# Up-projection of an FFN with seven block products for eight, on one core of a Trainium2 chip

## The chip, the cores and the metric

The program runs on 1 core of one Trainium2 chip. The metric is the device time of one execution in microseconds. Five engines work side by side: TensorE (PE in the profile, its weight loads PEld), VectorE (DVE), ScalarE (ACT), GpSimd (POOL) and SyncE (SP, which here issues loads). Each carries out its own instructions in order; semaphores hold one back until another's result is there.

## The reference

One step of a trunk of two layers over 640 tokens, 512 latent ones and 128 of context. Each layer has a mixer (attention, mLSTM and spatial gating) and an FFN. The change is in the FFN, and in where the modulation vectors (shift, scale, gate) are computed:

```python
D_MODEL = 1024; D_FF = 2816
def dwconv3(x, w, b):
    T = x.shape[1]
    xp = jnp.pad(x, ((0, 0), (1, 1), (0, 0)))
    return xp[:, :T] * w[0] + xp[:, 1:T + 1] * w[1] + xp[:, 2:] * w[2] + b

def trunk_layer(x, cond, l, P, rope, ctx):
    mod = (jax.nn.silu(cond) @ P['w_mod'][l] + P['b_mod'][l])[:, None, :]
    sh1, sc1, g1, sh2, sc2, g2 = jnp.split(mod, 6, axis=-1)
    h = rmsnorm(x) * (1.0 + sc1) + sh1
    mix, ctx_out = token_mixer(h, l, P, rope, ctx)
    x = x + g1 * mix
    h = rmsnorm(x) * (1.0 + sc2) + sh2
    u = dwconv3(h @ P['w_up'][l], P['ffn_conv_w'][l], P['ffn_conv_b'][l])
    x = x + g2 * ((jax.nn.silu(u[..., :D_FF]) * u[..., D_FF:]) @ P['w_down'][l])
    return x, ctx_out
```

## The kernel before

Activations lie feature by token: 128 features on the partitions, 640 tokens along the free axis, eight such tiles for the 1024 features. Each float32 operand of a large product is split into a high part (rounded to the matmul's float32 form) and a low part (the rest), and a product is three matmuls: high by high, high by low, low by high. `mm` runs over the feature tiles, these three terms and two halves of 320 tokens, so an output tile of 128 rows takes 8 x 3 x 2 = 48 matmuls of 320 columns. `weights` loads a tile's weights (tag `raw`), lets ScalarE round them to `whi` (line 104), and GpSimd and VectorE in turn subtract to get `wlo` (line 105); there are three `raw` buffers and four each of `whi` and `wlo`.

The FFN's up-projection has 44 output tiles, two to each of 22 pairs `f` (one under SiLU, one that multiplies it). `up` makes a pair: 96 matmuls into two accumulators in PSUM, each read by `conv` (ScalarE's pass at line 181, and four `scalar_tensor_tensor` of VectorE at lines 183 and 185, for 511 and 127 columns, which read the accumulator `acc` and add into the SBUF tile `cw`). `glu` then applies SiLU (line 964), multiplies on GpSimd (line 965) and splits the product into `act` tiles (lines 114 and 115). After each of three groups of pairs (`FFN_PARTS`) the down-projection adds that group's share to the residual `x`.

A modulation part is 512 columns of `w_mod` times the two condition vectors: eight loads issued by ScalarE, 16 narrow matmuls (line 290), four transposes (line 310). `mod_turn` places a part between bulk matmuls. Before, six parts run in the first layer's mixer and fourteen in its FFN, which include those of the second layer.

The order of the instructions on each engine is set when the program is built, by a scheduler that goes by its own estimate of time; calls marked `pin` keep the order in which the code is written.

## Time and profile before

| | |
|---|---|
| median of 3 runs | 2408.47 us (2407.22 to 2408.69) |
| the profiled execution | 2406.03 us, its span 2404.2 us |
| TensorE busy | 2369.4 us (99%) |
| VectorE busy | 1129.8 us (47%) |
| ScalarE busy | 950.2 us (40%) |
| GpSimd busy | 670.4 us (28%) |

The span runs from the first instruction to the last. A busy time is the time in which the engine had at least one instruction running; matmuls overlap in its pipeline, so their mean duration (310 ns) is longer than the distance between two. An instruction that waits for a port of the memory counts as busy.

### The profile page before, as it was taken

What the parts mean: (1) busy time and instruction counts of PE and PEld (TensorE: products, weight loads), DVE (VectorE), ACT (ScalarE), POOL (GpSimd) and SP (SyncE); (2) the same over time, 40 slices, a digit from 0 to 9 for tenths busy, and PEclk for the clock granted to TensorE, in tenths of its full rate; (3) what the DMA queues carried; (4) which work ended last, traced back from release to release, by engine and by line L of the source; (5) the groups of instructions that cost most, each with busy time, mean ns of one, the idle gap of its engine ahead of it and who ended that gap; (6) DMA issues with size and microseconds to landing.
All of it is one profiled execution on the core that took longest, in us unless ns stands there. A gap on an engine that the chain in (4) does not pass through costs nothing.

```text
span 2404.2 us, 40627 instructions
## 1 busy us (share of the span) xinstructions
PE 2369.4 (99%) x16708; PEld 2314.0 (96%) x16708; DVE 1129.8 (47%) x2102; ACT 950.2 (40%) x1737; POOL 670.4 (28%) x486
## 2 busy tenths in 40 slices
PE   8999999999999999999999999999999999999998
PEld 7999999999998999989999999999999999999998
DVE  5455535555246423424453555365544454243444
ACT  4432325455345323323354323254553543232334
POOL 2312222333322322313313222323324133232231
PEclk9999999999999999999999999999999999999999
DMA  9331251112241455452232222211112322222222
GB/s 317 106 106 58 72 165 66 64 63 67 74 150 62 138 171 174 136 171 77 84 103 72 72 66 67 69 56 63 63 53 72 117 67 74 76 78 72 80 71 70
DMA packets 88761, 227.39 MB, mean 95 GB/s; under 512 B 9472, under 2 KB 23936, under 8 KB 88576
## 3 DMA queue, kind: packets, MB, share of 16 engines
q1 hardware_dynamic: 68992, 189.14, 24.0%
q10 hardware_dynamic: 19584, 35.66, 4.3%
q8 instruction: 131, 2.15, 0.4%
q14 instruction: 54, 0.44, 0.1%
HBM read 217.41 MB, written 7.35 MB: 93 GB/s over the span
## 4 chain that ended last, share of the span: by engine, by line
PE 95%; DVE 3%; ACT 1%; issue 0%; DMA 0%; SPq 0%; DVEq 0%; ACTq 0%; POOL 0%; POOLq 0%
PE acc L133 78%; PE acc L174 6%; PE ms L290 2%; PE ms L920 2%; PE ms L891 2%; PE ms L174 1%; PE ms L913 1%; PE ms L765 1%; PE ms L754 1%; PE ms L767 1%; DVE x L488 0%; PE ms L719 0%; PE ms L585 0%; PE ms L310 0%; DVE h L405 0%
## 5 line engine op out<-in xcount | busy, mean ns | idle before, releaser
L133 PE MATMUL acc<-h,whi 128*128 128x320 f32 x6464 | 1247.1, 311 | 8.9 <-DVE h L405 5.1
L133 PEld LDWEIGHTS acc<-h,whi 128*128 128x128 f32 x6464 | 1021.0, 188 | 26.4 <-DVE h L405 9.1
L105 POOL TENSOR_TENSOR wlo<-raw,whi 128x512 fp32r<-128x512 f32 (+1 forms) x298 | 390.3, 1310 | 1323.4 <-ACT whi L104 1308.6
L133 PE MATMUL acc<-h,wlo 128*128 128x320 f32 x3232 | 757.8, 310 | 0.0
L104 ACT CAST whi<-raw 128x512 fp32r<-128x512 f32 x596 | 365.1, 614 | 993.4 <-PE acc L133 724.5
L133 PEld LDWEIGHTS acc<-h,wlo 128*128 128x128 f32 x3232 | 545.6, 188 | 0.1
L105 DVE TENSOR_TENSOR wlo<-raw,whi 128x512 fp32r<-128x512 f32 (+1 forms) x298 | 241.3, 810 | 469.2 <-ACT whi L104 430.2
L133 PE MATMUL acc<-act,whi 128*128 128x320 f32 x1408 | 269.3, 310 | 0.0
L133 PEld LDWEIGHTS acc<-act,whi 128*128 128x128 f32 x1408 | 221.9, 188 | 5.9 <-issue 5.9
L133 PE MATMUL acc<-act,wlo 128*128 128x320 f32 x704 | 165.8, 310 | 0.0
L548 DVE SCALAR_TENSOR_TENSOR x<-acc,mod,x 128x128 f32<-128x128 f32 (+3 forms) x136 | 66.3, 526 | 190.8 <-PE acc L133 190.8
L133 PE MATMUL acc<-y,whi 128*128 128x320 f32 x768 | 150.7, 312 | 1.4 <-DVE y L118 1.4
L174 PE MATMUL acc<-whi,h 128*128 128x256 f32 x768 | 145.7, 284 | 0.0
L183 DVE SCALAR_TENSOR_TENSOR cw<-acc,vec,cw 128x511 f32<-128x511 f32 (+1 forms) x176 | 95.7, 544 | 98.4 <-ACT cw L181 97.1
L174 PEld LDWEIGHTS acc<-whi,h 128*128 128x128 f32 x768 | 123.1, 192 | 0.8 <-ACT v L817 0.8
L133 PEld LDWEIGHTS acc<-y,whi 128*128 128x128 f32 x768 | 121.4, 188 | 2.0 <-DVE y L118 1.9
L133 PEld LDWEIGHTS acc<-act,wlo 128*128 128x128 f32 x704 | 119.0, 188 | 0.0
L965 POOL TENSOR_TENSOR cw<-cw,cw 128x640 f32<-128x640 f32 x44 | 69.4, 1578 | 155.9 <-DVE cw L185 155.9
L174 PE MATMUL acc<-wlo,h 128*128 128x256 f32 x384 | 108.9, 284 | 0.0
L185 DVE SCALAR_TENSOR_TENSOR cw<-acc,vec,cw 128x511 f32<-128x511 f32 (+1 forms) x176 | 96.7, 550 | 6.1
L133 PE MATMUL acc<-y,wlo 128*128 128x320 f32 x384 | 90.2, 313 | 0.0
L899 ACT ACTIVATE wk<-ms,mx 128x640 f32<-128x640 f32 (+1 forms) x80 | 56.7, 709 | 75.0 <-DVE mx L897 73.1
(256 smaller groups left out, 2385.8 us busy)
## 6 DMA issues: line engine op xcount, KB each, us to landing
raw<-w_in_f SPq DMA_DIRECT2D x98, 512.0 KB, 3.3
raw<-w_up SPq DMA_DIRECT2D x88, 512.0 KB, 3.3
mw<-w_mod ACTq DMA_DIRECT2D x104, 256.0 KB, 5.6
raw<-w_down SPq DMA_DIRECT2D x32, 448.0 KB, 3.4
raw<-w_in_v SPq DMA_DIRECT2D x24, 512.0 KB, 3.7
raw<-w_branch SPq DMA_DIRECT2D x24, 512.0 KB, 3.3
mw<-w_mod SPq DMA_DIRECT2D x16, 512.0 KB, 8.8
raw<-w_out SPq DMA_DIRECT2D x16, 512.0 KB, 3.2
```

Source lines behind the costliest of these rows:

```text
L104: nc.scalar.copy(hi, raw[:, a:b])
L105: self.alt().tensor_sub(lo, raw[:, a:b], hi.bitcast(F32))
L133: ins = nc.tensor.matmul(acc[:, s], a[:, sl], b[:, s], start=k == 0 and i == 0, stop=k == last and i == 2)
L174: self.queue(nc.tensor.matmul(accs[b], a[:, bs], w[:, sl], start=first and b % 2 == 0, stop=last and (b % 2 == 1 or b == NB - 1)))
L183: nc.vector.scalar_tensor_tensor(dst[:, a + 1 : b], acc[:, a : b - 1], w0, dst[:, a + 1 : b], ALU.mult, ALU.add)
L185: nc.vector.scalar_tensor_tensor(dst[:, a : b - 1], acc[:, a + 1 : b], w2, dst[:, a : b - 1], ALU.mult, ALU.add)
L290: ins = nc.tensor.matmul(ps[j : j + 32, 0:width], self.cs[:, k, :], raws[k], start=k < 4, stop=k >= 4, tile_position=(0, j))
L548: self.nc.vector.scalar_tensor_tensor(x[:, a:b], acc[:, a:b], g[:, k, i : i + 1], x[:, a:b], ALU.mult, ALU.add)
L891: nc.tensor.matmul(ps[:, s : s + 320], st[:, qs], kk[:, s : s + 320], start=i == 0, stop=i == 1)
L899: nc.scalar.activation(e[:, 0:nk], ps[:, 0:nk], AF.Exp, bias=mx, scale=scale, accum_out=sm[:, j : j + 1])
L920: nc.tensor.matmul(po, at[:, c * P : (c + 1) * P], vv, start=c == 0, stop=c == n - 1)
L965: nc.gpsimd.tensor_mul(cs[0], cs[0], cs[1])
```

## The change

The pairs 3 to 21 of each layer (38 in all) are computed by Strassen's algorithm: the two output tiles, the two halves of the 1024 features and the two halves of the tokens make blocks of two by two, and seven block products of 4 x 3 = 12 matmuls of 320 columns (`quarter`) take the place of eight. The seven weight blocks are the tiles' quarters or sums of them (`ws`, made by VectorE and GpSimd), each split by `halves`; the token factors (`tx`) are made once in a layer by `token_factors`, from the normalized activations, while the pairs 1 and 2 are computed as before. The products are collected from PSUM into two SBUF tiles `cw`, and `conv` now reads these instead of the accumulators. The down-projections come after four groups of pairs instead of three, their first two tiles interleaved. No modulation part runs in an FFN any more: all stand in the mixers and the output projections. The layer's constants move to the mixer's memory pool.

```diff
-FFN_PARTS = ((0, 7), (7, 14), (14, 22))
+FFN_PARTS = ((0, 5), (5, 11), (11, 16), (16, 22))
...
+    def quarter(self, acc, w, xs, first, last):
+        nc = self.nc
+        hi, lo = w
+        for k, (xh, xl) in enumerate(xs):
+            sl = slice(k * P, (k + 1) * P)
+            for i, (a, b) in enumerate(((hi, xh), (hi, xl), (lo, xh))):
+                ins = nc.tensor.matmul(acc, a[:, sl], b, start=first and k == 0 and i == 0, stop=k == 3 and i == 2,
+                                       skip_group_check=not first)
+                self.queue(ins, True)
+
+    def halves(self, src, eng=None):
...
+        if eng is None:
+            nc.scalar.activation(hi, src, AF.Identity, scale=-1.0)
+            nc.vector.scalar_tensor_tensor(lo, src, -1.0, hi.bitcast(F32), ALU.mult, ALU.subtract)
+        else:
+            nc.scalar.copy(hi, src)
+            eng.tensor_sub(lo, src, hi.bitcast(F32))
+        return hi, lo
+
+    def seven_front(self, st, b):
+        nc, p = self.nc, st["p"]
+        (a11, a12), (a21, a22) = st["r"]
+        w1 = self.halves(a11, nc.vector)
+        w2 = self.halves(a12, nc.gpsimd)
+        s1, s2, s3 = (self.t(p, [P, 512], F32, "ws") for _ in range(3))
+        nc.vector.tensor_add(s1, a21, a22)
+        nc.gpsimd.tensor_add(s2, s1, a11)
+        nc.vector.tensor_add(s3, a11, a21)
+        st["s"] = s1, s2, s3
+        self.quarter(st["x"], w1, b["11"], True, False)
+        nc.scalar.copy(st["c"][0][:, 0:NHALF], st["x"])
+        self.quarter(st["y"], w2, b["21"], True, True)
+        nc.vector.tensor_add(st["c"][0][:, 0:NHALF], st["y"], st["c"][0][:, 0:NHALF])
+
+    def seven_mid(self, st, b):
...
+        w6 = self.halves(s2, nc.gpsimd)
+        w5 = self.halves(s1, nc.vector)
+        w7 = self.halves(s3, nc.gpsimd)
+        nc.gpsimd.tensor_add(s2, s2, a12)
+        self.quarter(x, w6, b["t2"], False, False)
+        nc.scalar.copy(c0[:, NHALF:NT], x)
+        self.quarter(z, w5, b["t1"], True, False)
+        self.quarter(x, w7, b["t3"], False, False)
+        nc.scalar.copy(c1[:, NHALF:NT], x)
+        nc.vector.scalar_tensor_tensor(c1[:, NHALF:NT], z, -1.0, c1[:, NHALF:NT], ALU.mult, ALU.subtract)
+
+    def seven_back(self, st, b):
...
+        w4 = self.halves(st["r"][1][1])
+        w3 = self.halves(st["s"][1], nc.gpsimd)
+        self.quarter(st["x"], w4, b["t4"], False, True)
+        nc.scalar.mul(c1[:, 0:NHALF], st["x"], -1.0)
+        self.quarter(st["z"], w3, b["22"], False, True)
+        nc.vector.tensor_add(c0[:, NHALF:NT], st["z"], c0[:, NHALF:NT])
+        return c0, c1
...
+        def make(k):
+            u0, u1 = u[k], u[k + 4]
+            f0, f1 = (self.t(p, [P, NHALF], F32, "ws") for _ in range(2))
+            (a0, a1, _), (p0, p1, _) = cols
+            self.tc.keep_in_program_order(nc.vector.tensor_sub(f0[:, a0], u0[:, a0], u0[:, a1]))
+            nc.vector.scalar_tensor_tensor(f0[:, p0], u0[:, p0], d0[:, k : k + 1], u0[:, p1], ALU.add, ALU.subtract)
+            for c0, c1, g in cols:
+                nc.vector.scalar_tensor_tensor(f1[:, c0], u1[:, c1], sh[:, k + 4, g : g + 1], f0[:, c0],
+                                               ALU.add, ALU.add)
+            parts("t2", f1)
+            parts("t1", f0)
...
+        def flush():
+            for f, st in pending:
+                glu([conv(2 * f + i, c) for i, c in enumerate(self.seven_back(st, b))])
+            pending.clear()
+
+        def up7(f):
+            st = self.seven_open(p2, [self.I["w_up"][l, i] for i in (2 * f, 2 * f + 1)])
+            self.seven_front(st, b)
+            flush()
+            self.seven_mid(st, b)
+            pending.append((f, st))
+
         glu([conv(i, acc) for i, acc in enumerate(accs)])
+        b, make, finish = self.token_factors(p2, h, u, self.mods[l, 3])
+        make(0)
+        make(1)
+        up(1)
+        make(2)
+        make(3)
+        up(2)
+        finish()
+        done = 3
         st = self.norm_open(l + 1, 0 if nxt else None, p2, "cw")
         for f0, f1 in FFN_PARTS:
-            for f in range(len(acts), min(f1 + 1, NF)):
-                up(f)
-                if f % 2 == 0:
-                    self.mod_turn((p2, "mw", 1))
+            for f in range(done, min(f1 + 1, NF)):
+                up7(f)
+                done = f + 1
+            end = f1 == NF
+            flush()
...
-                    self.mod_todo = [] if l else [(l, s, n) for s in (2, 3, 4) for n in range(2)]
+                    self.mod_todo = [(l, s, n) for s in (2, 3, 4, 5) for n in range(2)]
+                    if l + 1 < self.L:
+                        self.mod_todo += [(l + 1, s, n) for s in (0, 1) for n in range(2)]
```

VectorE, one pair of the up-projection in the first layer. Before, a pair (here the accumulators 9654 and 9719) has two low parts, eight operations of the convolution and every second time an activation's low part:

```order
L105 TENSOR_TENSOR wlo_9798<-raw_9791,whi_9797 128x512
L183 SCALAR_TENSOR_TENSOR cw_9713<-acc_9654,vec_7_90,cw_9713 128x511
L185 SCALAR_TENSOR_TENSOR cw_9713<-acc_9654,vec_7_90,cw_9713 128x511
L183 SCALAR_TENSOR_TENSOR cw_9713<-acc_9654,vec_7_90,cw_9713 128x127
L185 SCALAR_TENSOR_TENSOR cw_9713<-acc_9654,vec_7_90,cw_9713 128x127
L105 TENSOR_TENSOR wlo_9863<-raw_9856,whi_9862 128x512
L183 SCALAR_TENSOR_TENSOR cw_9778<-acc_9719,vec_7_90,cw_9778 128x511
L185 SCALAR_TENSOR_TENSOR cw_9778<-acc_9719,vec_7_90,cw_9778 128x511
L183 SCALAR_TENSOR_TENSOR cw_9778<-acc_9719,vec_7_90,cw_9778 128x127
L185 SCALAR_TENSOR_TENSOR cw_9778<-acc_9719,vec_7_90,cw_9778 128x127
```

Of the change, the end of one pair's convolution (the first five of its eight operations stand ahead of these rows) and what follows up to the next pair's first low part. The weights `raw_9626` and `raw_9627` are those of the pair at work, `raw_9474` belongs to the pair before it, and the sums `cw_9326` and `cw_9327` to the one before that:

```order
L325 SCALAR_TENSOR_TENSOR cw_9555<-cw_9326,vec_7_90,cw_9555 128x127
L325 SCALAR_TENSOR_TENSOR cw_9561<-cw_9327,vec_7_90,cw_9561 128x511
L195 TENSOR_TENSOR ws_9642<-raw_9627 128x512
L168 SCALAR_TENSOR_TENSOR wlo_9675<-raw_9474,whi_9674 128x512
L325 SCALAR_TENSOR_TENSOR cw_9561<-cw_9327,vec_7_90,cw_9561 128x127
L220 SCALAR_TENSOR_TENSOR cw_9480<-ms_9573,cw_9480 128x320
L197 TENSOR_TENSOR ws_9644<-raw_9626,raw_9627 128x512
L202 TENSOR_TENSOR cw_9632<-ms_9631,cw_9632 128x320
L171 TENSOR_TENSOR wlo_9732<-ws_9642,whi_9731 128x512
L115 TENSOR_TENSOR act_9570<-cw_9555,act_9569 128x640
L230 TENSOR_TENSOR cw_9479<-ms_9573,cw_9479 128x320
L171 TENSOR_TENSOR wlo_9788<-raw_9779,whi_9787 128x512
```

The convolution now reads `cw` and stands two pairs behind the weights; three low parts, two sums and three operations out of PSUM (`ms`) stand beside it.

GpSimd at the same places. Before, two pairs:

```order
L105 TENSOR_TENSOR wlo_8303<-raw_8300,whi_8302 128x512
L105 TENSOR_TENSOR wlo_8368<-raw_8365,whi_8367 128x512
L965 TENSOR_TENSOR cw_8222<-cw_8222,cw_8287 128x640
L105 TENSOR_TENSOR wlo_8477<-raw_8470,whi_8476 128x512
L105 TENSOR_TENSOR wlo_8542<-raw_8535,whi_8541 128x512
L965 TENSOR_TENSOR cw_8358<-cw_8358,cw_8423 128x640
L115 TENSOR_TENSOR act_8432<-cw_8358,act_8431 128x640
```

Of the change, one pair, and the first row of the next:

```order
L171 TENSOR_TENSOR wlo_9639<-raw_9626,whi_9638 128x512
L196 TENSOR_TENSOR ws_9643<-ws_9642,raw_9626 128x512
L171 TENSOR_TENSOR wlo_9679<-ws_9490,whi_9678 128x512
L1112 TENSOR_TENSOR cw_9555<-cw_9555,cw_9561 128x640
L171 TENSOR_TENSOR wlo_9728<-ws_9643,whi_9727 128x512
L214 TENSOR_TENSOR ws_9643<-ws_9643,raw_9626 128x512
L171 TENSOR_TENSOR wlo_9736<-ws_9644,whi_9735 128x512
L171 TENSOR_TENSOR wlo_9792<-raw_9779,whi_9791 128x512
```

Two low parts of a pair have become four, with two additions between them.

VectorE at the beginning of the first layer's FFN. Before, the convolution of the first pair (accumulator 7660) is followed by that of the second (7864):

```order
L183 SCALAR_TENSOR_TENSOR cw_7852<-acc_7660,vec_7_90,cw_7852 128x127
L185 SCALAR_TENSOR_TENSOR cw_7852<-acc_7660,vec_7_90,cw_7852 128x127
L105 TENSOR_TENSOR wlo_8008<-raw_8001,whi_8007 128x512
L183 SCALAR_TENSOR_TENSOR cw_7923<-acc_7864,vec_7_90,cw_7923 128x511
L185 SCALAR_TENSOR_TENSOR cw_7923<-acc_7864,vec_7_90,cw_7923 128x511
```

Of the change, where the first half of the token factors follows the same convolution:

```order
L325 SCALAR_TENSOR_TENSOR cw_8036<-acc_7861,vec_7_90,cw_8036 128x127
L244 TENSOR_TENSOR tfd_8048<-mod_193_1129 128x4
L246 TENSOR_TENSOR tfe_8050<-mod_193_1129 128x8
L264 TENSOR_TENSOR ws_8052<-cw_7215 128x192
L265 SCALAR_TENSOR_TENSOR ws_8052<-cw_7215,tfd_8048 128x128
L267 SCALAR_TENSOR_TENSOR ws_8053<-cw_7561,mod_193_1129,ws_8052 128x192
L265 SCALAR_TENSOR_TENSOR ws_8073<-cw_7287,tfd_8048 128x128
L267 SCALAR_TENSOR_TENSOR ws_8053<-cw_7561,mod_193_1129,ws_8052 128x128
L273 SCALAR_TENSOR_TENSOR cw_7561<-cw_7561,tfe_8050,cw_7215 128x192
L273 SCALAR_TENSOR_TENSOR cw_7561<-cw_7561,tfe_8050,cw_7215 128x128
L275 SCALAR_TENSOR_TENSOR cw_7561<-cw_7561,mod_193_1129,ws_8053 128x320
L264 TENSOR_TENSOR ws_8073<-cw_7287 128x192
```

Sixteen such operations and one weight low part now stand between that convolution and the next one, which frees an accumulator.

## Rows read from the trace of the kernel before

**Rows 1.** The page: busy us, share of the span, instructions.

```profile
PE 2369.4 (99%) x16708; PEld 2314.0 (96%) x16708; DVE 1129.8 (47%) x2102; ACT 950.2 (40%) x1737; POOL 670.4 (28%) x486
```

**Rows 2.** Chain of waits in order of time: start us, us, engine and line.

```profile
1940.44 445.51 PE acc L133 x3036
```

**Rows 3.** Busy time by window, four pairs of the second layer's up-projection.

```profile
core 0: us, PE busy (x) PEld busy (x) DVE busy (x) ACT busy (x) POOL busy (x), PEclk, DMA share, GB/s
1945.00:2001.32 56.32, 56.32 (x386) 56.32 (x385) 26.16 (x42) 21.33 (x32) 18.68 (x14) 1.00 0.24 75
```

**Rows 4.** Timeline of TensorE where one half's products follow one another.

```profile
715.74 0.46 PE L133 MATMUL acc<-h,whi 128*128 128x320 f32 x2
716.03 0.31 PE L133 MATMUL acc<-h,wlo 128*128 128x320 f32 x1
716.17 0.46 PE L133 MATMUL acc<-h,whi 128*128 128x320 f32 x2
716.47 0.31 PE L133 MATMUL acc<-h,wlo 128*128 128x320 f32 x1
716.62 0.46 PE L133 MATMUL acc<-h,whi 128*128 128x320 f32 x2
```

**Rows 5.** Groups by line and form, second layer's FFN: busy us, mean ns.

```profile
L105 POOL TENSOR_TENSOR wlo<-raw,whi 128x512 fp32r<-128x512 f32 x54 | 70.1, 1298 | 186.1 <-ACT whi L104 186.1
L104 ACT CAST whi<-raw 128x512 fp32r<-128x512 f32 x107 | 66.4, 620 | 220.3 <-PE acc L133 174.8 <-issue 45.3
L181 ACT ACTIVATE cw<-acc,vec 128x640 f32<-128x640 f32 x40 | 35.2, 880 | 0.0
L965 POOL TENSOR_TENSOR cw<-cw,cw 128x640 f32<-128x640 f32 x20 | 31.6, 1578 | 70.7 <-DVE cw L185 70.7
L183 DVE SCALAR_TENSOR_TENSOR cw<-acc,vec,cw 128x511 f32<-128x511 f32 x40 | 29.9, 747 | 53.3 <-ACT cw L181 52.9
L183 DVE SCALAR_TENSOR_TENSOR cw<-acc,vec,cw 128x127 f32<-128x127 f32 x40 | 13.6, 340 | 0.0
```

**Rows 6.** Timeline of the first layer's up-projection: start us, us, engine.

```profile
795.84 0.69 DVE L105 TENSOR_TENSOR wlo<-raw,whi 128x512 fp32r<-128x512 f32 x1 [4.13 <-ACT whi L104]
...
798.90 1.58 POOL L965 TENSOR_TENSOR cw<-cw,cw 128x640 f32<-128x640 f32 x1 [5.29 <-DVE cw L185]
...
799.36 1.66 DVE L105 TENSOR_TENSOR wlo<-raw,whi 128x512 fp32r<-128x512 f32 x1 [0.61 <-ACT whi L104]
...
802.87 1.30 POOL L105 TENSOR_TENSOR wlo<-raw,whi 128x512 fp32r<-128x512 f32 x1 [2.39 <-ACT whi L104]
...
803.61 0.75 DVE L183 SCALAR_TENSOR_TENSOR cw<-acc,vec,cw 128x511 f32<-128x511 f32 x1 [1.52 <-ACT cw L181]
```

**Rows 7.** Instructions by tile: ns min/median/max, and the forms.

```profile
L420 DVE TENSOR_TENSOR cw<-cw,ms x48: 469/479/489, 726.4 to 1933.7; 128x320 f32<-128x320 f32 x48
L405 DVE SCALAR_TENSOR_TENSOR h<-cw,mod,h x72: 338/413/1230, 727.6 to 1935.1; 128x320 fp32r<-128x320 f32 x24, 128x192 fp32r<-128x192 f32 x24, 128x128 fp32r<-128x128 f32 x24
L414 POOL TENSOR_TENSOR act<-cw,act x4: 862/870/874, 2390.0 to 2398.4; 128x320 f32<-128x320 f32 x4
```

**Rows 8.** Timelines of GpSimd and VectorE in the second layer's mixer.

```profile
1800.11 3.69 POOL L788 TENSOR_TENSOR hs<-hs,dasum 128x640 f32<-128x640 f32 x2 [4.48 <-DVE dasum L786]
1802.61 1.74 DVE L105 TENSOR_TENSOR wlo<-raw,whi 128x512 fp32r<-128x512 f32 x1
1803.77 1.74 POOL L105 TENSOR_TENSOR wlo<-raw,whi 128x512 fp32r<-128x512 f32 x1
```

**Rows 9.** Timeline of TensorE at a modulation part in the first FFN.

```profile
809.31 0.60 PE L310 MATMUL ms<-ident,modev 128*128 128x128 f32 x4
809.83 1.92 PE L290 MATMUL ms<-mw,cs 128*32 128x512 f32 x16
811.69 0.70 PE L133 MATMUL acc<-h,whi 128*128 128x320 f32 x3
```

**Rows 10.** Busy time by window (clock after POOL) and TensorE's timeline after the handoff.

```profile
738.00:745.00 7.00, 5.82 (x33) 4.58 (x33) 7.00 (x21) 5.02 (x14) 0.00 (x0) 1.00 0.00 0
745.00:748.60 3.60, 3.60 (x16) 3.60 (x16) 0.88 (x3) 1.40 (x2) 1.26 (x1) 0.53 0.00 0
...
745.87 0.74 PE L133 MATMUL acc<-h,whi 128*128 128x320 f32 x2
...
746.67 0.74 PE L133 MATMUL acc<-h,whi 128*128 128x320 f32 x2
```

More of the change, by code (lines that the diff above doesn't have):

```diff
@@ new lines, in seven_back, with token_factors, parts, finish @@
+    def seven_back(self, st, b):
+        nc = self.nc
+        c0, c1 = st["c"]
+        w4 = self.halves(st["r"][1][1])
[5 more added lines that the diff above has]
+        return c0, c1
+    def token_factors(self, p, h, u, sh):
+        nc = self.nc
+        half = (slice(0, NHALF), slice(NHALF, NT))
+        cols = [(slice(c, d), slice(NHALF + c, NHALF + d), g) for c, d, g in ((0, NS - NHALF, 0), (NS - NHALF, NHALF, 1))]
+        b = {n: [] for n in ("11", "21", "22", "t1", "t2", "t3", "t4")}
+        for k in range(4):
+            for n, kk, t in (("11", k, 0), ("21", k + 4, 0), ("22", k + 4, 1)):
+                b[n].append(tuple(x[:, half[t]] for x in h[kk]))
+        d0 = self.t(self.sp, [P, 4], F32, "tfd", 1)
+        self.tc.keep_in_program_order(nc.vector.tensor_sub(d0, sh[:, 0:4, 0], sh[:, 0:4, 1]))
+        d1 = self.t(self.sp, [P, 4, 2], F32, "tfe", 1)
+        self.tc.keep_in_program_order(nc.vector.tensor_sub(d1, sh[:, 4:8, :], sh[:, 0:4, :]))
+        todo = []
+        def parts(n, src):
+            hi, lo = (self.t(p, [P, NHALF], F32R, "tx") for _ in range(2))
+            if n == "t2":
+                nc.scalar.activation(hi, src, AF.Identity, scale=-1.0)
+                nc.vector.scalar_tensor_tensor(lo, src, -1.0, hi.bitcast(F32), ALU.mult, ALU.subtract)
+            else:
+                nc.scalar.copy(hi, src)
+                nc.gpsimd.tensor_sub(lo, src, hi.bitcast(F32))
+            b[n].append((hi, lo))
+        def make(k):
[9 more added lines that the diff above has]
+            parts("t1", f0)
+            for c0, c1, g in cols:
+                nc.vector.scalar_tensor_tensor(u1[:, c1], u1[:, c1], d1[:, k, g : g + 1], u0[:, c1], ALU.add,
+                                               ALU.subtract)
+            nc.vector.scalar_tensor_tensor(u1[:, half[0]], u1[:, half[0]], sh[:, k + 4, 0:1], f1, ALU.add,
+                                           ALU.subtract)
+            parts("t4", u1[:, half[0]])
+            todo.append((k, u1[:, half[1]]))
+        def finish():
+            for k, src in todo:
+                hi, lo = (x[:, half[1]] for x in h[k])
+                nc.scalar.copy(hi, src)
+                self.alt().tensor_sub(lo, src, hi.bitcast(F32))
+                b["t3"].append((hi, lo))
+        return b, make, finish
@@ L334, in mod_turn @@
             self.mod_held = None
[L336 removed]
+        if src:
+            self.mod_load(src, self.nc.scalar)
     def mod_close(self):
@@ L614, in mlstm_qk @@
         for i in (head, H + head):
+            if turn and i >= H:
+                self.mod_turn()
             acc = self.fm(l, T_MLQ + i, h)
@@ L953, in branch, with ffn @@
                 out.append(self.split(merged[m], self.hp, "h", scale=0.5))
+                if m == KD - 2:
+                    self.mod_turn()
+        if last:
+            self.mod_close()
         return out
-    def ffn(self, l, h, accs, x, p2, nxt):
+    def ffn(self, l, h, u, accs, x, p2, nxt):
         nc = self.nc
@@ L1095, in run @@
                     nxt = l + 1 < self.L
[L1096 to L1098 removed]
+                    h, accs = self.ffn(l, h2, st["u"], accs, x, tags, nxt)
                     if nxt:
```

102 lines of the change are left out of this document (62 added, 40 removed).

## The prediction

> **What bounds the kernel now.** I read the page's busy shares first: TensorE is busy for 99% of the span, VectorE for 47%, ScalarE for 40%, GpSimd for 28% [rows 1]. Then the chain of waits in order of time: from the start of the second layer's FFN to its last products it is one unbroken run of 3036 matmuls in 445.51 us, so a product of 320 columns costs 445.51 / 3036 = 146.7 ns and nothing else ends late there [rows 2]. The busy time by window shows four pairs of up-projection tiles (4 x 96 products x 146.7 ns = 56.3 us): TensorE 56.32 us, VectorE 26.16, ScalarE 21.33, GpSimd 18.68, or 6.5, 5.3 and 4.7 us for a pair of 14.08 us [rows 3]. So a product taken away is worth its 146.7 ns, as long as those three engines keep ahead. Whether they do is the question here.
>
> **What is removed.** A pair of tiles goes from 96 to 84 products. This is done for 19 pairs in each layer, 38 x 12 = 456 products: 456 x 146.7 ns = **-66.9 us** if nothing waits. The new products go one half of the tokens at a time into one accumulator; where the kernel already does that, six products stand 0.88 us apart, also 146.7 ns each [rows 4]. TensorE's pair becomes 84 x 0.1467 = 12.32 us.
>
> **What a pair adds to the other engines.** Instead of four weight splits it needs seven. ScalarE: seven casts of 0.62 us, two passes of 0.88 us for the convolution, SiLU, the cast of its product, and four copies out of PSUM for which no row exists; with 0.88 us for every one of these last six ScalarE has 7 x 0.62 + 8 x 0.88 = 11.4 us, still under 12.32 [rows 5].
>
> GpSimd has in its order four low parts and two additions of 512 columns, the product of 640, and every second low part of an activation: 6 x 1.30 + 1.5 x 1.58 = 10.2 us [rows 5]. VectorE has three low parts and two sums of 512 columns (5 x about 0.70 = 3.5 us, [rows 6] for 0.69), three operations out of PSUM (3 x 0.48 = 1.4, [rows 7]), half an activation's low part (0.4) and the eight convolution operations: 4 x 0.75 + 4 x 0.34 = 4.4 us [rows 5]. That is 9.7 us. Each alone fits into 12.32.
>
> They do not run alone. In the rows a VectorE operation with two operands in SBUF doesn't run while a GpSimd operation does: the low part takes 0.69 us by itself, and 1.66 us when it begins 0.46 us into a GpSimd product of 1.58 us; it ends 0.54 us after that product [rows 6]. It holds the other way too: in [rows 8] GpSimd ends at 1803.80, VectorE's waiting operation 0.55 us later, and GpSimd's next, started at 1803.77, only 1.16 us after that, taking 1.74 us for 1.30. So a waiting operation hides about 0.15 us of its own time, and the two take turns. An operation that reads PSUM is free: a convolution operation that begins during a GpSimd low part takes its normal 0.75 us [rows 6].
>
> That is why the convolution matters. Before, its eight operations read the accumulator in PSUM; now they read the assembled sum in SBUF, and their second operand was in SBUF already. All eight join those that exclude GpSimd. So 8.3 us of VectorE's 9.7 and all of GpSimd's 10.2 must take turns.
>
> VectorE, in its order, is the longer chain. In the order each GpSimd operation finds a VectorE operation waiting or running, and so stands once in VectorE's way, for its length less the hidden 0.3 us (0.15 us at either end): 6 x 1.0 + 1.5 x 1.28 = 7.9 us. While VectorE works from PSUM, 1.4 us, it isn't held. A pair then takes 9.7 + 7.9 - 1.4 = **16.2 us**. Bounds: if the turns leave no gap at all, the parts that exclude each other are 5.9 us (VectorE: 8.3 less 0.15 for each, 0.2 taken for the eight of the convolution) and 9.1 us (GpSimd: 7.5 operations, each less 0.15), 15.0 us; with nothing hidden 8.3 + 10.2 = 18.5 us. I take 16.2, since the order leaves GpSimd waiting for the first sum (line 195 after the convolution) while VectorE alone holds the pair up.
>
> The Trainium skill ("SBUF — State Buffer", section "Who interferes with whom") says that a VectorE instruction with two SBUF inputs and a GpSimd instruction that reads SBUF exclude each other, the later one blocked until the first is finished. Taken to the letter, whole instruction after whole instruction, it gives the 18.5 us, and 50 us more for the sum below than 16.2 does; the rows show the exclusion, but with 0.15 us hidden.
>
> Not every pair pays. The FFN has four stages of 3, 6, 5 and 5 such pairs, each followed by down-projections in which the three engines have little to do. VectorE's order has a pair's convolution two pairs later, so the first two pairs of each stage run at TensorE's 12.32 us: 1 + 4 + 3 + 3 = 11 pairs a layer pay 16.2 - 12.32 = 3.88 us, 22 x 3.88 = 85 us. The four weight buffers let the splits run up to three products (of 1.76 us) ahead when a stage begins; I take 3 us of that off for three of the stages in each layer, 18 us. **+67 us** (bounds 41 and 118: a contended pair of 15.0 and of 18.5 us).
>
> **Token factors.** Between the convolution of the first pair and that of the second VectorE now makes half the factors: per pair of feature tiles, six operations of 0.34 to 0.41 us and two of about 0.55, 3.3 us [rows 7], for two 6.7, with a low part 7.4 us, with some five of GpSimd's operations (0.87 us for 320 columns, [rows 7]) in the way, some 5 us more. The first accumulator of the second pair is full 7 us into it and has to be read before the third pair begins, at 14.1 us. VectorE comes to it at 4.4 (convolution of the first pair) + 7.4 + 5 = 16.8 and has read it at 19: 5 us of waiting for TensorE, and one more in the second half. **+12 us** for two layers; 0 if GpSimd is never in the way (14.0 us), 20 if it always is.
>
> **The rest.** Fourteen modulation parts leave the FFN of the first layer (a part took TensorE 811.69 - 809.31 = 2.4 us there, [rows 9]); six go ahead of it, eight into the second layer's mixer, with the same products between the same bulk matmuls: 0, taken as +2 for waits. The last pair of each layer must pass convolution, SiLU, product and split before the last down-projection, with 60 x 0.1467 = 8.8 us of products as cover and, by the durations above, some 10 us of work: +3. The sixteen extra residual operations lie under down-projections: 0.
>
> **Sum.** -66.9 + 67 + 12 + 5 = +17 us on the profiled execution's 2406.0 us; by the bounds -66.9 + 41 = -26 and -66.9 + 118 + 20 + 6 = +77. The runs' median is 2408.5, 2.4 above that execution, so I forecast **2426 us**. A difference under 0.2% (4.8 us) can't be told from none.
>
> **The rivals.** (1) TensorE stays the bound: the splits keep ahead after all, because GpSimd's operations fall into VectorE's idle times. Then only the token factors and ends remain: 2408.5 - 66.9 + 10 = 2352 us. For it: each engine alone fits. Against it: 15.0 us of turns in a pair of 12.32 even without a gap. It decides if a contended pair takes under about 12.5 us; 8%. (2) The turns come near their lower bound, or more of the queue drains in the down stages: a contended pair of 15.0 to 15.2 us, or up to 15.8 with the token factors hidden, ending at 2380 to 2403. The point from which it decides is a pair of about 15.4 us: 22 x 0.8 us is the whole forecast. 20%. (3) Within 4.8 us of before: 10%. (4) TensorE's clock falls as well. After a thin stretch at the handoff the granted clock was 0.53 of full for 3.6 us, and three products there take 0.80 us, 267 ns each, the 1.2 GHz level [rows 10]. A contended pair leaves TensorE idle for 3.9 us; if the clock stayed at the low level a pair would need 84 x 0.267 = 22.4 us, 22 x 6.2 = 136 us more, about 2560. Single falls hide in the idle time. 4%.
>
> The Trainium skill ("TensorE: Matmul & The Clock Gate", section "Why this matters for your kernels") asks for no long idle gaps between bursts of matmuls, which speaks for (4); the stage before has no such gap [rows 2, 3].
>
> **How the numbers follow.** My own case (a contended pair of 15.6 to 18.5 us, 2413 to 2485) has 58%. The range for 8 in 10 takes in most of (2) and of my case: 2376 to 2478; my own case alone would be 2413 to 2478. Faster by over 0.2%: (1) and (2), 0.28. Same: 0.10. Slower: 0.62.
>
> **What would show it.** In the profile after, in the pairs of the FFN: VectorE's convolution operations of 511 columns far over 0.75 us on average, its low parts over 0.69, GpSimd's over 1.30; products of the up-projection waiting on VectorE's and GpSimd's low parts; some 16 us between the first products of neighbouring pairs, 12.3 for the first of a stage; TensorE's count lower by 456. I am wrong if the convolution operations stay at 0.75 us, if a pair takes 12.3 us throughout, or if the time is lost in the mixers, whose stages I leave unchanged.

## The result and the profile after

The change is slower: 2505.59 us median of 4 runs (2504.67 to 2510.76) against 2408.43 us for the kernel before on the same chip, ratio 1.0409 (95% interval 1.0391 to 1.0427), 97 us where I forecast 17. The profiled execution took 2505.15 us, its span 2503.4 us.

The page after, busy time, share and instructions, to be read beside [rows 1]:

```profile
PE 2361.2 (94%) x16252; PEld 2272.1 (91%) x16252; DVE 1444.8 (58%) x2450; ACT 1082.5 (43%) x2067; POOL 959.0 (38%) x674
```

TensorE has the 456 products less, but its busy time fell by only 8.2 us. VectorE is busy for 315 us more and GpSimd for 289; the same 2450 instructions of VectorE take 1291.6 us, 153 less, in the kernel below that leaves out GpSimd's weight work. The groups by line and form show it (busy us, mean ns, then the idle time before them); [rows 5] has 747 ns for the same 511 columns, 1298 for GpSimd's low part:

```profile
L323 DVE SCALAR_TENSOR_TENSOR cw<-cw,vec,cw 128x511 f32<-128x511 f32 x76 | 88.6, 1166 | 5.7 <-ACT cw L321 5.7
L171 POOL TENSOR_TENSOR wlo<-ws,whi 128x512 fp32r<-128x512 f32 x114 | 171.6, 1509 | 44.4 <-ACT whi L170 44.4
```

One such meeting in the timelines of VectorE and GpSimd (start, us):

```profile
2184.22 1.78 DVE L323 SCALAR_TENSOR_TENSOR cw<-cw,vec,cw 128x511 f32<-128x511 f32 x1
...
2183.71 1.74 POOL L214 TENSOR_TENSOR ws<-ws,raw 128x512 f32<-128x512 f32 x1
```

The convolution operation begins with 1.23 us of GpSimd's addition to go and takes 1.78 us: those 1.23, and 0.55 of the 0.75 that it takes alone.

The last up-projection stage of the second layer by window, five pairs, cut at the first product of each pair (length, then busy us of TensorE, its weight loads, VectorE, ScalarE, GpSimd, then the granted clock, DMA share and GB/s). Before, TensorE was busy throughout such a stage [rows 3]:

```profile
2368.10:2376.90 8.80, 8.80 (x62) 8.80 (x61) 5.08 (x7) 3.76 (x7) 6.16 (x5) 1.00 0.17 60
2376.90:2389.22 12.32, 12.32 (x86) 12.32 (x85) 8.12 (x10) 7.29 (x13) 9.00 (x7) 1.00 0.25 87
2389.22:2404.34 15.12, 13.40 (x86) 12.33 (x85) 13.22 (x18) 8.23 (x15) 9.95 (x8) 1.00 0.21 70
2404.34:2419.93 15.59, 13.17 (x87) 12.37 (x86) 15.59 (x16) 8.33 (x15) 13.18 (x8) 1.00 0.19 67
2419.93:2444.50 24.57, 18.49 (x111) 17.44 (x110) 20.13 (x25) 11.27 (x21) 17.34 (x11) 0.93 0.22 65
```

Two pairs run free (the first has five products before the next pair's, 8.80 us), two take 15.1 and 15.6 us, and the last with its two late products takes 24.57 us where nine products of 1.76 us are 15.84. Over all eight stages TensorE loses 125.5 us (each stage's length, with a wait ahead of it, less its products at 146.7 ns). By the same cut, 45.8 us of that lie in the 14 pairs between the second and the last of the six later stages (13.9 to 17.7 us, 15.6 on average), 63.8 in the eight stage ends (21.0 to 26.0 us for 15.84), and 16.0 in the first stage of each layer: 9.9 in its first two pairs, which don't run free, the rest ahead of them. Some 19 us of the 125.5 come from products of 0.267 us at a granted clock of 0.5, the 1.2 GHz level, to which it falls 17 times in the program, 11 of them in these stages or just ahead of one; before, it fell 4 times.

For whom the new products and their weight loads waited, over the program (us, times; the two overlap and both are counted, of the products alone it is 27.0, 22.9 and 21.7 us):

```profile
  ACT cw L219: 58.0, 27
  POOL wlo L171: 54.6, 63
  ACT cw L216: 48.6, 33
```

L216 and L219 are ScalarE's copies out of the accumulator after P6 and P7 (the seven products are named after their weights, `w1` to `w7` in the code), without which the next product into it can't start. TensorE's waits in the stage end shown above, and the SiLU behind which the last of these copies stood on ScalarE:

```profile
2428.94 0.41 PE L157 MATMUL acc<-tx,wlo 128*128 128x320 f32 x1 [1.19 <-POOL wlo L171]
2434.32 0.57 PE L157 MATMUL acc<-h,whi 128*128 128x320 f32 x2 [1.89 <-ACT cw L216]
2439.29 0.56 PE L157 MATMUL acc<-tx,whi 128*128 128x320 f32 x2 [2.93 <-ACT cw L219]
...
2437.88 0.74 ACT L1111 ACTIVATE cw<-cw 128x640 f32<-128x640 f32 x1 [3.09 <-DVE cw L325]
```

The lengths of the stages (us). A norm has two groups of products `ms<-ones,sqa`, some 10 us apart; a stage runs from the second group of one norm to the first of the next, the first mixer from its first token-major product (`ms<-whi,h`):

| kernel | mixer and output 1 | FFN 1 | mixer and output 2 | FFN 2 |
|---|---|---|---|---|
| before | 670.9 | 498.2 | 669.8 | 464.3 |
| after | 703.7 | 498.0 | 703.2 | 501.8 |
| moved parts alone | 704.6 | 464.4 | 701.5 | 463.1 |
| no weight work on GpSimd | 703.8 | 444.8 | 702.7 | 445.9 |
| all weight parts on VectorE | 701.8 | 474.3 | 703.5 | 473.5 |

The first FFN lost 14 parts and 228 products, 67 us of TensorE's time, and still stayed as long; both mixers grew by 33 us.

### The profile page after: what moved, and what is told of

It reads as the page before. It is cut to its first block, busy times and chain, and to the rows that moved or that the text cites. A ratio compares the mean times of both kernels' runs of the same rounds, so it can differ in the third digit from the quotient of the medians.

```text
span 2503.4 us, 40883 instructions
## 1 busy us (share of the span) xinstructions
PE 2361.2 (94%) x16252; PEld 2272.1 (91%) x16252; DVE 1444.8 (58%) x2450; ACT 1082.5 (43%) x2067; POOL 959.0 (38%) x674
## 5 line engine op out<-in xcount | busy, mean ns | idle before, releaser
L133 PE MATMUL acc<-h,whi 128*128 128x320 f32 x4032 | 792.8, 312 | 15.8 <-DVE h L546 6.4
L133 PEld LDWEIGHTS acc<-h,whi 128*128 128x128 f32 x4032 | 638.7, 188 | 36.1 <-DVE h L546 10.8
L133 PE MATMUL acc<-h,wlo 128*128 128x320 f32 x2016 | 479.9, 311 | 0.0
L133 PEld LDWEIGHTS acc<-h,wlo 128*128 128x128 f32 x2016 | 341.6, 188 | 0.0
L105 DVE TENSOR_TENSOR wlo<-raw,whi 128x512 fp32r<-128x512 f32 (+2 forms) x238 | 172.6, 725 | 263.1 <-ACT whi L104 260.0
L171 POOL TENSOR_TENSOR wlo<-ws,whi 128x512 fp32r<-128x512 f32 x114 | 171.6, 1509 | 44.4 <-ACT whi L170 44.4
L157 PE MATMUL acc<-tx,whi 128*128 128x320 f32 x608 | 141.7, 320 | 31.5 <-ACT cw L219 27.0
L157 PE MATMUL acc<-h,whi 128*128 128x320 f32 x608 | 141.6, 321 | 27.8 <-ACT cw L216 21.7
L157 PE MATMUL ms<-h,whi 128*128 128x320 f32 x608 | 140.3, 318 | 0.0
L157 PEld LDWEIGHTS acc<-tx,whi 128*128 128x128 f32 x608 | 104.3, 194 | 36.6 <-ACT cw L219 30.9
L157 PEld LDWEIGHTS acc<-h,whi 128*128 128x128 f32 x608 | 105.0, 195 | 33.4 <-ACT cw L216 26.9
L323 DVE SCALAR_TENSOR_TENSOR cw<-cw,vec,cw 128x511 f32<-128x511 f32 (+1 forms) x152 | 131.9, 909 | 5.7 <-ACT cw L321 5.7
```

Source lines behind the costliest of these rows:

```text
L105: self.alt().tensor_sub(lo, raw[:, a:b], hi.bitcast(F32))
L133: ins = nc.tensor.matmul(acc[:, s], a[:, sl], b[:, s], start=k == 0 and i == 0, stop=k == last and i == 2)
L157: ins = nc.tensor.matmul(acc, a[:, sl], b, start=first and k == 0 and i == 0, stop=k == 3 and i == 2, skip_group_check=not first)
L171: eng.tensor_sub(lo, src, hi.bitcast(F32))
L323: nc.vector.scalar_tensor_tensor(dst[:, a + 1 : b], acc[:, a : b - 1], w0, dst[:, a + 1 : b], ALU.mult, ALU.add)
```

## The experiments

From the waits I formed three theories: (A) the turns of VectorE and GpSimd make VectorE late, and ScalarE's queue, in which operations wait for VectorE, passes it on to the two copies; (B) ScalarE's queue alone; (C) the turns alone, by which the weights' low parts come too late. The 107 us that an expectation below names for the copies count the weight loads as well; of the products alone it was 48.7 us. Differences below are to the runs of before on the same chip.

**Moved parts alone.** The changed kernel with the FFN of before:

```diff
-            st = self.seven_open(p2, ...)   # and all of up7, token_factors
+            acc = self.psA(); w = self.weights(self.I["w_up"][l, i], KD * P)
+            self.mm(acc, w, 0, h)
```

> The change without Strassen's algorithm: the FFN of before (96 products a pair, no token factors) in the changed kernel, with all modulation parts outside the FFN and the layer's constants in the mixer's pool as in the change. Prices the moved parts alone. My forecast's term for them was +2 us, that is 2410. By the stages of the trace after (both mixers with their output projections 33 us longer, the start 5 us shorter, 14 parts of 2.4 us = 34 us gone from the first FFN) it should be +28 us, that is 2432 to 2440, with both FFNs at about 464 us. If the FFN alone made the loss: 2404 to 2414.

2432.27 us, +22.5, ratio 1.0091 (1.0076 to 1.0106). The moved parts cost 22.5 us, not 2. TensorE's timeline at two places:

```profile
134.97 0.39 PE L314 MATMUL ms<-whi,h 128*128 128x256 f32 x1 [3.41 <-DVE mod L454]
...
148.94 1.92 PE L430 MATMUL ms<-mg,cs 128*32 128x512 f32 x16 [0.28 <-DVE mod L454]
...
158.47 4.13 PE L430 MATMUL ms<-mg,cs 128*32 128x512 f32 x16
```

A token-major product waits 3.41 us for the buffer of an earlier part, whose closing reduction stands behind the gates' scans on VectorE. A part 9.5 us behind the one before it takes 4.13 us for 1.92: its loads, issued from 151.15 us on, when its predecessor's buffers came free, were not all there (the last landed at 161.51). The 20 parts after the start took some 49 us of TensorE's time before and 61 here.

**GpSimd's weight work left out.**

```diff
+            if eng is nc.gpsimd:
+                return hi, hi
-        nc.gpsimd.tensor_add(s2, s1, a11)
-        nc.gpsimd.tensor_add(s2, s2, a12)
```

> Leaves out, in the Strassen pairs, GpSimd's four low parts and its two weight additions (the high part stands in for the low part, the first sum for the second; TensorE's products, ScalarE's casts and copies and VectorE's operations keep their number), so that of the exclusion between GpSimd and VectorE only the product and the activation's low part are left. Theory A (the exclusion makes VectorE and GpSimd late, and ScalarE's queue, in which the copies out of PSUM stand behind passes that wait for VectorE, hands it on to TensorE): the 125 us of waits in the pairs fall to 15 to 40, and the time to 2395 to 2425. Rival B (the order of ScalarE's queue alone, with its 11 us of work in a pair of 12.3): the waits at the copies stay, over 90 us, 2470 or more. Rival C (the exclusion alone, low parts too late): as A, 2385 to 2415.

2396.31 us, -13.5, ratio 0.9944 (0.9928 to 0.9961). TensorE's loss in the eight stages is 8.2 us. The same stage as above, the last four pairs:

```profile
2281.50:2293.82 12.32, 12.32 (x86) 12.32 (x85) 7.59 (x15) 7.77 (x14) 0.00 (x0) 1.00 0.23 75
2293.82:2306.14 12.32, 12.32 (x86) 12.32 (x85) 9.00 (x18) 8.56 (x16) 1.58 (x1) 1.00 0.25 84
2306.14:2318.46 12.32, 12.32 (x86) 12.32 (x85) 8.97 (x17) 8.56 (x16) 3.16 (x2) 1.00 0.25 85
2318.46:2335.10 16.64, 16.12 (x110) 15.86 (x109) 11.09 (x18) 10.71 (x21) 5.08 (x4) 1.00 0.20 60
```

VectorE's 17 or 18 instructions of a full pair take 9.0 us, where 16 to 18 took 13.2 to 15.6 in the change; the clock stays full; the stage's end takes 16.64 us. ScalarE works as much as in the change (1088.6 us busy for 1082.5), so B falls. The edit leaves out more than turns: the second sum is the first (`s2 = s1`), so the chain over GpSimd's two additions is gone, and four of a pair's low parts need no buffer.

**The two copies freed.**

```diff
-        nc.scalar.copy(c0[:, NHALF:NT], x)
+        nc.scalar.copy(c0[:, NHALF:NT], a11[:, 0:NHALF])
```

and the same for `c1`.

> Leaves out the reading of the accumulator at two points: the two ScalarE copies (after the products P6 and P7) copy a weight tile instead, so that TensorE's next products into that accumulator don't wait for them; ScalarE does as much as before, in the same queue. Theory A: of the 107 us that TensorE waited for those two copies about two thirds are saved and the rest reappears at the low parts of GpSimd, which the exclusion keeps late: 2425 to 2455. Rival B: nearly all of it is saved, 2400 to 2415. Rival C: TensorE waits as long, now for the low parts: 2490 to 2505.

2503.70 us, +93.9. The time stays. The waits moved (products and weight loads again; of the products alone 39.8 and 19.4 us):

```profile
  POOL wlo L171: 86.4, 52
  ACT whi L170: 45.2, 48
```

So A, which I held by then, falls too: the copies were in the main only the last to be late. Not altogether: the stage ends lose 38.7 us for 63.8. But the pairs as a whole lose only 12 less, and 10 of these come back in the down-projections, so that the two FFNs are 2.4 us shorter. C is left.

**Another order of the products**, P1 P2 P6 P4' P5 P3' P7 (the dash: of the pair before).

```diff
         nc.scalar.copy(c0[:, NHALF:NT], x)
+        if prev: self.seven_p4(prev, b)
         self.quarter(z, w5, b["t1"], True, False)
+        if prev: self.seven_p3(prev, b)
```

> The whole computation, with TensorE's seven products in another order: the two last products of the pair before stand between P6 and P5 and between P5 and P7, so that one to two more products of 1.76 us lie between each copy out of an accumulator and the next product into it. The last pair of a stage still ends P7, copy, P4, P3. Theory A: the copies of the middle pairs come in time, part of their some 48 us of waits goes to the low parts, the ends of the stages (some 64 us) stay: 2475 to 2490. Rival B: 2450 to 2465. Rival C: no change, 2500 to 2510.

2577.77 us, +168.0, which no theory had. The copies are in time now (5.0 us of the products' waits), but P4 comes earlier than its low part, which the scheduler left behind six convolution operations on VectorE:

```profile
2235.45 0.64 PE L157 MATMUL acc<-tx,wlo 128*128 128x320 f32 x1 [4.06 <-DVE wlo L168]
```

The products wait 85.3 us for that low part. So this order tells nothing of theory A against C.

**All weight parts on VectorE.**

```diff
-        w2 = self.halves(a12, nc.gpsimd)   # likewise w6, w7, w3
+        w2 = self.halves(a12, nc.vector)
-        nc.gpsimd.tensor_add(s2, s1, a11)  # likewise s2 + a12
+        nc.vector.tensor_add(s2, s1, a11)
```

> The whole computation; in the Strassen pairs the four low parts and two weight additions of GpSimd are made by VectorE, which gets six more operations a pair. Theory C (the exclusion alone): GpSimd's operation of 1.3 us or more is replaced by one of about 0.72 us in the same turn, VectorE works 9.0 + 6 x 0.72 = 13.3 us a pair and gives way only to GpSimd's product and half a low part, so a pair comes to 14.0 to 14.6 us instead of about 15.5: 2460 to 2485, and VectorE's operations go back to the lengths that they have alone. If instead the load of VectorE as such is the bound (13 to 14 us of 15 busy in the change), six more operations make a pair some 4 us longer: 2580 to 2600.

2452.26 us, +43.8: 53 us faster than the change. The whole last stage by window, first of the change and then of this kernel:

```profile
2368.10:2444.50 76.40, 66.18 (x423) 63.26 (x422) 62.14 (x73) 38.88 (x71) 55.62 (x36) 0.98 0.21 69
```

```profile
2323.90:2391.30 67.40, 62.93 (x423) 61.62 (x422) 58.08 (x101) 38.92 (x70) 13.60 (x7) 1.00 0.26 79
```

VectorE carries out 28 more instructions in 4 us less, so the load of VectorE as such was not the bound. This run alone doesn't tell its turns with GpSimd from GpSimd's slower operations (1.3 us for 0.7); the convolution with one operand and the pair of kernels with a shared buffer, below, do: GpSimd's work stays whole there, and the time falls with VectorE's part of the turns.

**Every second pair or so by eight products.**

```diff
-                up7(f)
+                (up7 if f in (3, 5, 6, 9, 10, 12, 14, 15, 18, 19) else up)(f)
```

> The whole computation; only 10 of the 19 pairs of a layer are made by 7 products, the others by 8 as before, at most two in a row; the down-projections come in five stages of up to five instead of four, and the third feature block's factor has its own buffer, for memory. Theory C: a Strassen pair wants 17 us of turns of VectorE and GpSimd and an ordinary one under 7, together less than the 26.4 us that TensorE needs for both, so that the waits nearly vanish: 2432 (the moved parts) - 20 x 1.76 + some 25 for the token factors and the shorter stages = 2420 to 2445. If every Strassen pair costs its wait wherever it stands (125 us / 38 = 3.3 us each): 2480 to 2495.

2437.67 us, +29.2. As C has it, within its 2420 to 2445: a stage of two Strassen and two ordinary pairs runs without a gap:

```profile
2246.40:2299.20 52.80, 52.80 (x362) 52.80 (x361) 29.06 (x49) 26.64 (x45) 29.07 (x21) 1.00 0.26 78
```

**The convolution with one operand.**

```diff
-            nc.vector.scalar_tensor_tensor(dst, acc, w0, dst, ALU.mult, ALU.add)
+            nc.vector.tensor_scalar_mul(dst, acc, w0)
```

(The column ranges are left out here and in the next block; all eight operations are changed alike.)

> Leaves out the addition in the eight convolution operations of the Strassen pairs: each multiplies its columns by its weight and writes them over the result, so it reads one operand from SBUF instead of two (about 0.54 us for 0.80). GpSimd's work stays whole. My prediction's own step (the convolution, moved from PSUM to SBUF, is what joins the exclusion): these operations no longer give way to GpSimd, the turns left are 4.2 us of VectorE and some 10 of GpSimd, the waits fall from 125 us to under 40, 2400 to 2430. If operations with one SBUF operand take turns as well, VectorE only saves its 1.5 us a pair: 2465 to 2480. If GpSimd's amount of work (10 us a pair and the chain behind it) were the cause by itself: 2490 to 2505.

2468.91 us, +60.4, 37 us faster than the change: the second case, and not the third (GpSimd's amount of work by itself, 2490 or more). VectorE's and GpSimd's timelines:

```profile
1054.66 1.52 DVE L1126 TENSOR_SCALAR cw<-cw,vec 128x511 f32<-128x511 f32 x1
...
1054.16 1.75 POOL L171 TENSOR_TENSOR wlo<-ws,whi 128x512 fp32r<-128x512 f32 x1
```

Alone such an operation takes 0.48 us (mean of the 102 that meet no GpSimd operation); here 1.52. It begins with 1.25 us of GpSimd's operation to go. So it takes turns with one SBUF operand as well. The Trainium skill ("SBUF — State Buffer", section "Who interferes with whom") lists `tensor_scalar` among those that can take the pair of ports shared with GpSimd; the run agrees. Only its shorter time was gained.

**The convolution with an operand in PSUM**, and its control.

```diff
-        st["x"] = self.t(self.ps, [P, 1024], F32, "acc", 2)[:, 0:NHALF]
+        xz = self.t(self.ps, [P, 1024], F32, "acc", 2)   # both kernels
+        st["x"], st["z"] = xz[:, 0:NHALF], xz[:, 512 : 512 + NHALF]
-                nc.vector.scalar_tensor_tensor(dst, acc, w0, dst, ...)
+                nc.vector.scalar_tensor_tensor(dst, still, w0, dst, ...)   # the first
```

> The eight convolution operations of the Strassen pairs take their first operand from a constant PSUM buffer instead of the assembled sum, so the two outer taps of the convolution are left out; number, columns and second operand stay, and two accumulators share a buffer to make room. It sets the convolution back to one operand in PSUM, as before the change. My prediction's step (the convolution's move from PSUM to SBUF is what joins the exclusion): VectorE's turns fall from 8.3 to 4.2 us a pair, its convolution operations go back to 0.75 and 0.34 us whether GpSimd works or not, waits under 40 us of 125: 2400 to 2425. If the weights' additions and low parts alone make the turns: 2460 or more.

2562.17 us, +154.0: slower, where I expected 2400 to 2425. By tile, the operations on 511 and 127 columns together (ns min/median/max):

```profile
L1127 DVE SCALAR_TENSOR_TENSOR cw<-ms,vec,cw x152: 336/540/752, 841.9 to 2498.1; 128x511 f32<-128x511 f32 x76, 128x127 f32<-128x127 f32 x76
```

With line 1128 there are 304 of them. None takes over 0.752 us, and 152 overlap a GpSimd operation; in the change the same line reaches 1.85 us. The mechanism is as I had it. The time is not: TensorE's products wait 99 us for the copies out of the shared buffer (219 with the weight loads, the figure in the next expectation). Hence the control, which shares the buffer but convolves the sum in SBUF:

> The whole computation: the control for the kernel whose convolution took an operand from PSUM (2562 us). The two accumulators of a pair share one buffer as there, the convolution reads the assembled sum in SBUF as in the change. If the sharing alone made that kernel slow (TensorE waited 219 us there for the copies out of the shared buffer) and the convolution's exclusion adds to it: 2590 to 2640. If the copies set the pair by themselves, whatever the convolution reads: 2555 to 2570.

2591.96 us, +185.2: 31 us more than its partner, with the same work on GpSimd. So the convolution's move to SBUF does cost, beside the waits of the shared buffer; what it costs in the change itself these two don't tell.

**Token factors made and never used.**

```diff
-                up7(f)
+                up(f)   # and t3 in buffers of its own, five stages
```

> The token factors are made and never used: all pairs of the FFN are made by 8 products as before, in five stages as in the mixed kernel, with the moved parts. Prices the token factors with the shorter stages. My forecast's term for the factors was +12 us, on top of the 2432 of the moved parts: 2444. If the opening of the FFN costs what the kernel without GpSimd's weight work shows (about 7 us a layer) and the shorter stages nearly nothing: 2445 to 2450. If the 40 us that the mixed kernel lost beside its removed products (2437.7 = 2432.3 - 35.2 + 40.6) lie here: 2465 to 2475; if they lie at its Strassen pairs: 2440 to 2450.

2464.90 us, +56.7, 34 more than the moved parts alone. The opening of the second FFN by window, up to the first down-projection, here and with the moved parts alone:

```profile
1969.20:2046.80 77.60, 70.39 (x459) 68.45 (x458) 56.46 (x110) 37.97 (x72) 33.01 (x25) 0.98 0.17 55
```

```profile
1952.00:2065.10 113.10, 110.79 (x748) 109.27 (x747) 56.20 (x104) 48.37 (x80) 37.81 (x27) 1.00 0.20 68
```

456 and 744 products need 66.90 and 109.14 us, so 10.7 and 4.0 us are lost: the factors' own price is 6.7 us in this layer, by the same cut 7.2 in the first. The down-projections take some 6.2 us a layer over their products, none with the moved parts alone, and 18 products more a layer, 2.6 us, stand ahead of the next norm. That makes 31.6 of the 34.

**These with the old order of the down-projections.**

```diff
-            pair = [(self.psA(), self.weights(...)) for m in range(2)]
+                acc = self.psA(); w = self.weights(...)   # one at a time
```

> The kernel with the token factors made and never used (2464.9 us), with the down-projections one accumulator at a time as before the change. If the 1.6 us by which TensorE waits at nearly every down-projection stage there come from opening two accumulators at once (both have to be read by the last pair's convolution first): 2448 to 2455, and what is left above 2432 is the price of the token factors, 16 to 22. If the down-projections wait for the activations instead: 2462 to 2467.

2459.97 us, +53.2: 3.5 us less, between the two. In both layers a down-projection stage's loss fell from about 1.6 to 0.2 us, 4.5 us a layer, so the order is what costs there; the median followed by 3.5. In the profiled execution, the fastest of the four, the first FFN is 8.6 us shorter and the second 0.8: their openings differ by 3 us the one way and the other.

**One turn moved, and one part closed early**, both on the kernel of the moved parts.

```diff
-        self.tm(l, 0, h, evac, turn)
+        self.tm(l, 0, h, evac)   # and turn() ahead of the second feature tile
```

> The kernel of the moved parts alone (FFN of before, 2432 us), with one of its turns moved: not between the two halves of the first token-major products, where a part's open PSUM buffer made TensorE wait 3.4 us and the granted clock fell, but after the first of the four feature tiles that follow. If that wait and the slow products behind it cost what the trace shows (5.3 us in each layer): 2420 to 2424. If the part only waits elsewhere: 2430 to 2434.

2445.94 us, +37.4, slower by 15 us. I had taken the wait to the wrong place: it belongs to the mLSTM's token-major products and stayed, and the moved part made a new one of 4.79 us:

```profile
85.52 0.52 PE L728 MATMUL ms<-lc,wk 128*128 128x128 f32 x2 [4.79 <-DVE wk L715]
142.06 0.39 PE L314 MATMUL ms<-whi,h 128*128 128x256 f32 x1 [3.35 <-DVE mod L454]
```

```diff
+        self.mod_close()
         part = self.gates(l, acc)
```

> The kernel of the moved parts alone (2432 us), with one line more: the part that is open when the mLSTM's gates begin is closed (transposes, VectorE's reduction) ahead of the gates and not after them, so that its PSUM buffer comes free before VectorE's scans. The wait of 3.4 us in the token-major products that follow, and the slow products behind it, 5.3 us a layer, should go: 2419 to 2424. If that wait has another cause (the evacuation by ScalarE): 2430 to 2434.

2423.38 us, +15.2 for 22.5; the wait of 3.4 us is gone. A third of the price of the moved parts was this.

**What could be taken away together.**

```diff
+                (up7 if f in (3, 5, 6, 7, 9, 10, 12, 14, 15, 16, 18, 19, 20) else up)(f)
+        self.mod_close()   # and all weight parts on VectorE, the old down order
```

> The whole computation, with what the runs so far point to put together: 13 of the 19 pairs of a layer by 7 products and never the last of a stage, five stages, all weight parts of those pairs on VectorE, the open modulation part closed ahead of the gates, and the down-projections one accumulator at a time as before the change. From 2423.4 (moved parts with that part closed) - 26 x 1.76 + 14 (token factors) + 5 to 10 of waits = 2396 to 2402, under the 2408 of before. If the down-projections' order is not what costs 1.6 us a stage: 2408 to 2415. If Strassen pairs cost their wait wherever they stand, 2430 or more.

2417.76 us, +11.0, ratio 1.0042 (1.0030 to 1.0055): the fastest whole computation with Strassen's algorithm here, still slower than before, and 16 us over my 2396 to 2402. 26 x 1.76 = 46 us of products are gone, but the FFNs, 460.9 and 458.9 us by the marks of the table above, are only 4 us shorter than with the moved parts alone. In the second one 22.9 us of products are gone; the up-projections lose 10.4 us more, 9.0 of them before the first down-projection, where the token factors are made, the down-projections take 5.6 us over their products again, and 18 products more (2.6 us) stand ahead of the norm. That leaves the 4.2 us. The handoff to the final norm waits for 3.8 us, 1.9 with the moved parts alone (engine and line waited for, us, times, longest):

```profile
PE ms L517 <- DVE sqa L499: 3.8, 1, 3.8
```

## Why the prediction was right or wrong

The direction held; the sum was too small by 80 us. The runs give a ledger by steps: moved parts +22.5; Strassen without GpSimd's weight work -36.0; that work +110.6 (2505.59 - 2408.43 + 13.45); together 97. The trace of the change gives another, for its two FFNs against those of the moved parts alone: products -66.9, losses in the pairs +119.2, at the openings +9.7, in the down-projections +6.9, and 12 products more a layer ahead of the next norm +3.5; together 72.4, and the FFNs are 72.3 us longer.

- **Products, -66.9:** right. 456 fewer, 12.32 us for a free pair.
- **The turns:** right as a mechanism, with 0.19 us hidden at a meeting where the rows had 0.15. GpSimd's six operations a pair cost 110.6 us, and the same work on VectorE half of that (43.8 + 13.5). A contended pair between the free ones and the last took 15.6 us on average, within my bounds and a little under the 16.2 I took: the 14 of them cost 45.8 us, for 54 in my sum.
- **"Not every pair pays", 22 pairs less a lead of 18 us:** this step failed, the largest miss, 125.5 us for 67. (a) My sum took the last pair of a stage as a contended pair like the others, 3.88 us, 31 for the eight; the eight ends lose 63.8 us, 8.0 each. The first two pairs of the later stages do run free, but their VectorE and GpSimd work is not gone: in the end shown above, the last of ScalarE's copies stands behind a SiLU that waited 3.1 us for VectorE's convolution of the pair before. With the copies freed the ends still lose 38.7 us, without GpSimd's weight work 6.2. (b) Of the 18 us taken off for a lead little shows: the middle pairs cost 8 us less than in my sum, the ends far more. (c) In the first stage of a layer the first two pairs pay as well, and TensorE waits ahead of them: 16.0 us in all, nothing in my sum.
- **ScalarE "not binding":** right for the program's time: the list of waits names its copies first, but with the copies freed the time stayed within 4 us.
- **The last pair of each layer, +3:** of that size: the last down-projection takes 1.5 us over its products in each layer.
- **Token factors, +12:** about right: 13.9 us in the kernel that makes them unused, 8.0 more at the openings in the one without GpSimd's weight work, 9.7 in the change (some 6 of it the wait ahead of the first stages, which is in the 125.5 too). **Residuals and down-projections, 0:** wrong. They take 3.5 us a layer over their products in the change, 5.3 in the kernel without GpSimd's weight work. In that kernel the 10.6 of both layers, 8.0 at the openings, 8.0 in the pairs and 3.5 for the 12 products more a layer make 30.1 of the 30.9 between -66.9 and -36.0.
- **Moved parts, +2:** failed. I counted products and no waits. 22.5 us: by the timeline 12 are parts that take TensorE longer, as where loads come late when parts follow 10 us apart; by the run that closes a part early 7.3 are a PSUM buffer held by a part whose closing stood behind the gates' scans. The rest is not located.
- **"Single falls hide in the idle time" (rival 4):** half wrong. The clock didn't stay low, but its falls cost about 19 us of slow products in the pairs, which are part of the 125.5. They come with the waits: without GpSimd's weight work none lies in a stage of these pairs.

Of the signs I named, the convolution far over 0.75 us, the low parts over 0.69 and 1.30, pairs near 16 us and 12.3 at the start of the later stages came. Products waiting on low parts came by half: 22.9 us on GpSimd's, 2.2 on VectorE's, and 48.7 on ScalarE's copies, which I hadn't named. "The time is lost in the mixers", my sign for being wrong, came as well, for 22.5 of the 97 us.

Open: how much of the 110.6 us the convolution's move to SBUF makes and how much the weights' operations; how much of the 53 us that the weights' move to VectorE gained is turns saved and how much shorter operations; and why the down-projections' waits came back in the last kernel.

## What to carry to other kernels

Where two engines take turns, as these did, count them as one: add their times, and compare the sum with the bounding engine's time for the whole stage. A lag in the pipeline only delays that bill to the stage's end (63.8 us here). A list of waits names what was late last, not what made it late: take the wait away before believing it. Moving work to the faster of the two can help even if it is the busier; and a step that is moved is priced with its loads, its buffers and the queue behind which it closes.

## What the runs showed of the hardware that I had not expected

A VectorE operation with a single SBUF operand took turns with GpSimd too (`tensor_scalar`, 511 columns: 0.48 us alone, 1.52 us behind 1.25 us of a GpSimd operation), while one with an operand in PSUM never did (0.752 us at most). The turns are sharp: in the change, each of the 83 convolution operations that began behind a GpSimd operation took the rest of that operation and its own time alone (0.74 or 0.34 us) less 0.19 us; those that began 0.19 us or more ahead of GpSimd's took no longer than alone. And VectorE finished 101 instructions in 58.08 us where, beside 36 of GpSimd, 73 had taken 62.14.
